# Loading the second block's x behind the first weights, low halves on VectorE, and new transfer durations in a planned decoder layer

## Chip, cores and metric

The kernel runs on one core of a Trainium2 chip. The metric is the device time of one execution in microseconds (us).

## What is computed

One decoder layer on x (2048 x 1024, float32), cut to what matters here:

```python
a = rmsnorm(h, attn_norm)                          # d_model 1024
proj = einsum('bsd,de->bse', a, w_in)              # dq, dk, dv, sq, sk, sv: 512 columns each
diff_o = diff_attn(...)                            # 4 heads, softmax(q1 k1) - lam * softmax(q2 k2)
sb_o = stick_breaking(...)                         # 8 heads, products of (1 - beta) along the keys
h = h + concat(norm(diff_o), norm(sb_o)) @ w_out
m = rmsnorm(h, mlp_norm)
h = h + square(relu(m @ w_up)) @ w_down            # d_ff 4096
out = rmsnorm(h, final_norm)
```

Each float32 operand of a dense product is split into a high and a low half (both float32r), and a product is the three matmuls high x high, high x low, low x high. So every weight tile and every x tile is first split: ScalarE (ACT) copies the rounded high half, another engine subtracts it from the raw tile and leaves the low half.

## The kernel before

The sequence is cut into four blocks of 512 columns, taken in the order 3, 2, 1, 0. `emit_qkv((3, 2), ...)` (lines 641 to 654) makes the projections of blocks 3 and 2, weight by weight: `ORDER` lists 16 tiles of w_qk and 4 steps of w_v, and for the first three tiles (`lag` 3) all of block 3 comes ahead of all of block 2. Attention on these blocks follows, mixed with the projections of blocks 1 and 0, then the output product and the MLP of each block.

- `split_w` (537 to 555) loads a raw weight tile of 128 x 1024 (`x` in the profile), makes its two split tiles (`w`: 512 columns of high halves, 512 of low ones) and stores both in DRAM (`d_w_qk`, `d_w_v`, ...), from where later blocks load them ready. The low half is made by POOL in pieces of 256 columns (line 552).
- `load_x` (577 to 582) loads a block's x as four tiles of 128 x 1024 (`b<-x_T`). `norm_x` (591 to 600) splits each half of such a tile: ACT makes the high half, DVE the low one (`b<-b,g_attn`). `rms` and `rms_row` (609 to 632) square the tiles, add them up, reduce them on PE (`r`) and make the row of reciprocal norms.
- `halves` (565 to 570) gives the tiles of an x block's halves, two views of 512 columns in each tile; `space` (584 to 587) adds half a tile for the block's row.
- `emit_qk` (662 to 679): `product` (24 matmuls of 128x512, `d<-b,w`), then DVE scales the result by the row (`y<-d,b`), ACT makes the high half, DVE the low one (`y<-y`), and two transfers store them.

No instruction is issued where the code calls it. The calls are recorded as units with their dependences, and `Plan.order` (201 to 417) lays them out with a list scheduler in a model of the five engines, with durations from `Plan.duration` (160 to 198). A transfer holds SP for the returned 0.42, moves `u.bytes` at a rate by its row length after the transfers ahead of it, and lands 2.2 after its begin plus that move (lines 365 to 369; all in us). Which spot of SBUF a tile takes, and when, follows from `homes`, `MOST` and `LEAST` (421 to 424, 463 to 465). Dense units may run at most `AHEAD` = 100 ahead of the oldest open one. The order is then issued engine by engine; on the chip each engine and the SP queue take their instructions strictly in that order. All calls go through line 447, so the profile gives them that line and they are told apart by tiles.

At the start the recorded order is: gains, the first weight tile, x of block 3, the other two first weights, constants (with `lqk`, the four lambda vectors), and x of block 2 inside `emit_qkv` at step 1 (`load_to(2)`, line 1079), split at step 2 (`norm_to`).

Two lines that the text speaks of:

```python
for i in range(0, BW, HW):                                                   # 551, in split_w
    pool.tensor_tensor(out=lo[:, i:i + HW], in0=r[:, i:i + HW], ...)          # 552
finish = begin + 2.2 + u.moves                                               # 369, in Plan.order
```

Of the kernel before, what the change touches and what calls it, by code (L numbers as in the profile page):

```python
# [28 lines left out]
P = 128  # L29
# [77 lines left out]
class Plan:  # L107
# [52 lines left out]
    def duration(self, eng, method, kw, out, ins, u):  # L160
# [35 lines left out]
        u.bytes = math.prod(out.shape) * 4  # L196
        u.moves = u.bytes / {P: 265e3, HW: 300e3, BW: 335e3, D: 360e3}.get(row, 200e3)
        return 0.42


    def order(self, slots, phase_of, caps, log=None):
# [101 lines left out]
        while done < len(units):  # L303
# [14 lines left out]
            while progress:  # L318
                progress = False
                for e in avail:  # L320
# [3 lines left out]
                    for u in waiting[e]:  # L324
                        if u.ready > now + 1e-9:
                            continue
                        k = self.key(u, now)
                        if best is not None and k >= best[0]:
                            continue
                        if u.stream == "dense" and u.i > dense[at_dense].i + self.AHEAD:  # L330
                            continue
                        spots, ok = [], True
                        for t in u.allocs:
                            if queue[u.stream, self.line(t)][-1] is not t:
                                ok = False
                                break
                            s = place(t, now)
                            if s is None:
                                ok = False
                                break  # L340
                            spots.append((t, s))
                            if len(u.allocs) > 1:
                                free[s[0]].remove(s[1])
                        if len(u.allocs) > 1:
                            for t, s in spots:
                                free[s[0]].append(s[1])
                        if ok:
                            best = k, u, spots
# [16 lines left out]
                    if e == "SP":  # L365
                        avail[e] = now + u.dur
                        begin = max(now + 0.1, dma_free)
                        dma_free = begin + u.moves
                        finish = begin + 2.2 + u.moves
                    else:  # L370
                        finish = start + u.dur
                        avail[e] = finish
                        if e == "PE":
                            if now > self.pe_end + 0.05:
                                gaps.append((now - self.pe_end, now, u))
                            self.pe_end = finish
# [13 lines left out]
                    for s in u.succ:  # L390
                        s.ndeps -= 1
                        s.ready = max(s.ready, finish if s.eng == e else res + (0.04 if s.eng == "POOL" else 0.0))
                        if not s.ndeps:
                            waiting[s.eng].append(s)
                            heapq.heappush(events, s.ready)
                            if s.eng == "PE":
                                heapq.heappush(events, s.ready + self.MARGIN)
                    for t in users.get(id(u), ()):
                        t.left -= 1
# [18 lines left out]

    MARGIN, AHEAD, pe_end = 0.4, 100, 0.0

# [11 lines left out]
    def key(self, u, now):  # L432
# [3 lines left out]
        if u.eng == "SP":  # L436
            return (u.stream == "dense", u.frac if u.stream != "dense" else u.n)

# [13 lines left out]
def layer_kernel(ctx: ExitStack, tc: tile.TileContext, a: dict, out: bass.AP):  # L452
# [9 lines left out]
    TINY = dict(rvx=2, rrx=2, rx=4, rvh=2, rrh=2, negm=2, l=2, gam=2, rl=2, mm=2, left=8)  # L462
    homes = {"be": ["early", "xp"], "we": ["early"], "ye": ["early"], "xe": ["early"], "e": ["e", "e2"], "bx": ["xp"], "b": ["late", "xp"], "w": ["late", "xp"], "y": ["late", "xp"],
             "x": ["late", "xp"], "wm": ["xp"], "ym": ["m", "xp"], "xm": ["xp"], "yq": ["m", "xp"], "wq": ["xp"]}
# [72 lines left out]
    def split_w(name, *at):  # L537
# [9 lines left out]
        for j, t in enumerate(tiles):  # L547
            r, hi, lo = raw[:, j * BW:(j + 1) * BW], t[:, 0:BW], t[:, BW:D]
            act.activation(out=hi, in_=r, func=ACTF.Copy)

            for i in range(0, BW, HW):
                pool.tensor_tensor(out=lo[:, i:i + HW], in0=r[:, i:i + HW], in1=hi[:, i:i + HW].bitcast(F32), op=ALU.subtract)
            kept[name, at].append(dt(f"d_{name}_{'_'.join(map(str, at))}_{j}", [P, D]))
# [11 lines left out]
    def halves(last=False):  # L565
# [3 lines left out]
        h = h[0::2], h[1::2]  # L569
        return h, ([h[0][k // 2][:, k % 2] for k in range(KD)], [h[1][k // 2][:, k % 2] for k in range(KD)], b_)  # L570

# [12 lines left out]
    def space(last=False):  # L584
        n = len(rows) % 2
        rows.append(rows[-1] if n else buf(last=last))
        return halves(last) + (rows[-1][:, n * BW:(n + 1) * BW],)
# [3 lines left out]
    def norm_x(xs, where):  # L591

        tiles, views, row = where
        for kp, x in enumerate(xs):
            for k in range(2):
                g = g_attn[:, 2 * kp + k:2 * kp + k + 1]
                x_, hi, lo = x[:, k * BW:(k + 1) * BW], tiles[0][kp][:, k], tiles[1][kp][:, k]
                act.activation(out=hi, in_=x_, func=ACTF.Copy, scale=g)
# [431 lines left out]

    nxt = {}

# [26 lines left out]
    for i, n in enumerate(("lambda_q1", "lambda_k1", "lambda_q2", "lambda_k2")):  # L1059
# [18 lines left out]

    emit_qkv((3, 2), xs, 3, {1: load_to(2), 2: norm_to(2, False), 12: load_to(1), 13: norm_to(1, True),
                             16: load_to(0), 18: norm_to(0, True)}, ws)  # L1080
# [25 lines left out]
    slots.update(m=["m0", "m1"], e2=[f"f{i}" for i in range(4)])  # L1106
    phases = {k: ["be", "we", "ye", "xe"] for k in [*ATT, "m"]}
    phases.update(e2=["yq", "ym"], late=list(ATT))
# [80 lines left out]
```

## Time and profile before

| | |
|---|---|
| median of 3 runs | 2978.68 us (2973.56 to 2979.01) |
| the profiled execution | 2972.79 us, of which 2971.0 us is the span from first to last instruction |
| PE matmul busy | 2892.6 us, 97% of the span |
| DVE / ACT / POOL busy | 1767.4 (59%) / 1146.2 (39%) / 1099.7 us (37%) |
| DMA | 667.80 MB over one hardware queue, 67.5% of 16 engines' span |
| granted TensorE clock | 0.991 on average |

PE is TensorE, DVE is VectorE, POOL is GpSimd, SP issues all transfers. A row of the timeline gives start, length, engine, instruction, count, and in brackets how long the engine had been idle and what released it. A busy PE is modelled from pipelined matmuls.

### The profile page before, as it was taken

How to read it: one execution, taken by the hardware profiler on the slowest of the kernel's cores; microseconds unless marked ns; L12 is line 12 of the kernel's file. 1: busy time of each engine (PE TensorE's matmuls, PEld its weight loads, DVE VectorE, ACT ScalarE, POOL GpSimd, SP SyncE). 2: the span in 40 equal slices, each digit the busy share in tenths (PEclk: the TensorE clock that was granted, in tenths of full speed). 3: DMA queues.
4: the chain of work that ended last, by engine and by line, in shares of the span. 5: the costliest groups of instructions: out<-in, count | busy, mean ns of one | idle time of the engine just before them, and what ended most of it. 6: DMA issues, size and time to landing. Idle time of an engine off the chain costs nothing.

```text
span 2971.0 us, 42391 instructions
## 1 busy us (share of the span) xinstructions
PE 2892.6 (97%) x14928; PEld 2439.6 (82%) x14928; DVE 1767.4 (59%) x3193; ACT 1146.2 (39%) x2390; POOL 1099.7 (37%) x1589
## 2 busy tenths in 40 slices
PE   8999999999999999999999999999999999999997
PEld 6889789888887888788788888888888888888886
DVE  5243477777777888884588888887443333421112
ACT  4232255555655555663355555553120100211101
POOL 3221266554677787775344444543000000000000
PEclk9999999999999999999999999999999999999998
DMA  8776897777887877678866665654865556645551
GB/s 268 246 245 202 259 270 233 218 218 230 264 269 244 262 255 254 238 250 288 308 216 204 198 189 192 215 186 169 325 244 200 183 184 241 255 143 205 205 185 71
DMA packets 304164, 670.51 MB, mean 226 GB/s; under 512 B 26960, under 2 KB 121424, under 8 KB 303952
## 3 DMA queue, kind: packets, MB, share of 16 engines
q1 hardware_dynamic: 303952, 667.80, 67.5%
q8 instruction: 119, 1.95, 0.3%
q14 instruction: 93, 0.76, 0.1%
HBM read 491.53 MB, written 176.16 MB: 225 GB/s over the span
## 4 chain that ended last, share of the span: by engine, by line
PE 88%; DMA 6%; DVE 2%; POOL 1%; issue 1%; ACT 1%; SPq 1%; POOLq 0%; DVEq 0%; ACTq 0%
PE d L447 43%; PE dn L447 23%; PE s L447 8%; PE pt L447 6%; PE os L447 4%; PE od L447 3%; DMA v<-d_dv 2%; DMA sq<-d_sq 1%; DMA b<-x_T 1%; SPq L447 1%; DMA qa<-d_dq 1%; DVE b L447 1%; PE r L447 0%; POOL set L447 0%; POOL w L447 0%
## 5 line engine op out<-in xcount | busy, mean ns | idle before, releaser
L447 PE MATMUL d<-b,w 128*128 128x512 f32 x5376 | 1300.9, 395 | 14.1 <-ACT b L447 11.7
L447 PEld LDWEIGHTS d<-b,w 128*128 128x128 f32 x5376 | 1005.3, 189 | 233.1 <-ACT b L447 12.3
L447 PE MATMUL dn<-y,w 128*128 128x512 f32 x3072 | 742.3, 394 | 1.5 <-DVE y L447 1.4
L447 PEld LDWEIGHTS dn<-y,w 128*128 128x128 f32 x3072 | 572.9, 188 | 129.1 <-DVE y L447 1.7
L447 DVE TENSOR_TENSOR b<-b,dn 128x512 f32<-128x512 f32 x416 | 284.8, 685 | 294.9 <-PE dn L447 289.7
L447 POOL TENSOR_TENSOR w<-x,w 128x256 fp32r<-128x256 f32 x384 | 321.8, 860 | 254.5 <-ACT w L447 190.0
L447 POOL TENSOR_TENSOR set<-ser 128x512 f32<-128x512 f32 (+2 forms) x320 | 308.4, 965 | 153.3 <-DVE ser L447 139.7
L447 POOL TENSOR_TENSOR rrx<-rvx,mhalf 128x4 f32<-128x4 f32 x12 | 13.0, 1085 | 880.6 <-DVE rvx L447 880.6
L447 ACT ACTIVATE d<-d 128x512 f32<-128x512 f32 x128 | 74.9, 585 | 596.2 <-DVE d L447 595.8
L447 DVE SCALAR_TENSOR_TENSOR d<-d,b 128x512 f32<-128x512 f32 x128 | 89.3, 698 | 345.8 <-PE d L447 338.2
L447 DVE TENSOR_TENSOR_SCAN ser<-set,left 128x512 f32<-128x512 f32 x192 | 271.8, 1419 | 4.1 <-POOL set L447 3.0
L447 ACT ACTIVATE e<-e,negm 128x512 f32<-128x512 f32 (+3 forms) x320 | 210.5, 658 | 144.3 <-DVE negm L447 134.2
L447 ACT ACTIVATE hb<-pt 128x512 fp32r<-128x512 f32 (+1 forms) x320 | 163.7, 533 | 228.4 <-PE pt L447 135.9
L447 DVE TENSOR_TENSOR hb<-pt,hb 128x512 fp32r<-128x512 f32 (+1 forms) x320 | 186.6, 603 | 54.1 <-ACT hb L447 49.7
L447 DVE CUSTOM_DVE_ANT_0 e<-s,bias 128x512 f32<-128x512 f32 (+3 forms) x320 | 191.4, 598 | 39.4 <-PE s L447 38.9
L447 POOL TENSOR_SCALAR set<-set 128x512 f32<-128x512 f32 (+1 forms) x160 | 120.5, 754 | 240.6 <-ACT set L447 240.2
L447 ACT ACTIVATE set<-s 128x512 f32<-128x512 f32 (+1 forms) x320 | 165.5, 535 | 106.4 <-PE s L447 87.7
L447 PE MATMUL d<-w,b 128*128 128x256 f32 x1536 | 200.9, 285 | 3.3 <-DVE y L447 1.7
L447 PEld LDWEIGHTS d<-w,b 128*128 128x128 f32 x1536 | 190.5, 190 | 8.8 <-DVE y L447 5.1
L447 PE MATMUL s<-ka,qa 128*128 128x512 f32 (+3 forms) x640 | 178.5, 377 | 17.3 <-issue 8.2
L447 PE MATMUL os<-hb,sv 128*128 128x512 f32 (+3 forms) x640 | 186.3, 373 | 5.0 <-DVE hb L447 3.9
L447 PE MATMUL s<-ska,sq 128*128 128x512 f32 (+3 forms) x640 | 181.6, 379 | 7.6 <-DMA sq<-d_sq 3.8
(91 smaller groups left out, 3037.5 us busy)
## 6 DMA issues: line engine op xcount, KB each, us to landing
w<-d_w_up SPq DMA_DIRECT2D x192, 512.0 KB, 5.5
w<-d_w_down SPq DMA_DIRECT2D x192, 512.0 KB, 5.0
ka<-d_dk SPq DMA_DIRECT2D x80, 512.0 KB, 5.4
v<-d_dv SPq DMA_DIRECT2D x144, 256.0 KB, 4.3
d_w_up<-w SPq DMA_DIRECT2D x64, 512.0 KB, 5.4
d_w_down<-w SPq DMA_DIRECT2D x64, 512.0 KB, 6.2
w<-d_w_out SPq DMA_DIRECT2D x48, 512.0 KB, 6.9
ska<-d_sk SPq DMA_DIRECT2D x80, 256.0 KB, 4.1
```

The costliest lines, as they stand in the source:

```text
L447: fn(*[v.ap() if isinstance(v, View) else v for v in args], **{k: v.ap() if isinstance(v, View) else v for k, v in kw.items()})
```

## The change

- `load_x(2)` is recorded right behind the splits of the first three weights, instead of at step 1 of `emit_qkv`; `norm_to(2)` stays at step 2.
- While the weights' home is still the early one (all of `emit_qkv((3, 2), ...)`), their low halves are made by DVE, in one piece of 512 columns, instead of by POOL in two of 256. Later weights stay with POOL.
- The tile with the rows of blocks 3 and 2 gets a line of its own, `re`, in the early part of SBUF.
- `halves` cuts its views as plain column slices, whose columns the planner sees, where it did not through the rearranged views; `norm_x` uses these views.
- The planner's durations of a transfer: SP is held 0.48 instead of 0.42, the rates are some 6 to 11% lower, the landing is 2.6 instead of 2.2 behind.
- Three new numbers, `STORE`, `LOAD` and `EARLY`, enter the rules with values (0.0, 0.0, and 100 like `AHEAD`) that leave them as they were.

```diff
@@ -194,8 +194,8 @@
             return 0.19 + n * 0.00085
         row = min([out.shape[-1]] + [v.shape[-1] for v in ins])
         u.bytes = math.prod(out.shape) * 4
-        u.moves = u.bytes / {P: 265e3, HW: 300e3, BW: 335e3, D: 360e3}.get(row, 200e3)
-        return 0.42
+        u.moves = u.bytes / {P: 250e3, HW: 270e3, BW: 300e3, D: 320e3}.get(row, 200e3)
+        return 0.48
 
 
     def order(self, slots, phase_of, caps, log=None):
@@ -324,10 +324,12 @@
                     for u in waiting[e]:
                         if u.ready > now + 1e-9:
                             continue
+                        if e == "SP" and u.out.home is None and now < u.ready + self.STORE:
+                            continue
                         k = self.key(u, now)
                         if best is not None and k >= best[0]:
                             continue
-                        if u.stream == "dense" and u.i > dense[at_dense].i + self.AHEAD:
+                        if u.stream == "dense" and u.i > dense[at_dense].i + (self.AHEAD if len(self.seen) > 1 else self.EARLY):
                             continue
                         spots, ok = [], True
                         for t in u.allocs:
@@ -366,7 +368,7 @@
                         avail[e] = now + u.dur
                         begin = max(now + 0.1, dma_free)
                         dma_free = begin + u.moves
-                        finish = begin + 2.2 + u.moves
+                        finish = begin + 2.6 + u.moves
                     else:
                         finish = start + u.dur
                         avail[e] = finish
@@ -395,6 +397,9 @@
                             heapq.heappush(events, s.ready)
                             if s.eng == "PE":
                                 heapq.heappush(events, s.ready + self.MARGIN)
+                            if s.eng == "SP":
+                                heapq.heappush(events, s.ready + self.STORE)
+                                heapq.heappush(events, s.ready + self.LOAD)
                     for t in users.get(id(u), ()):
                         t.left -= 1
                         for kind in gate.get(t.home, ()):
@@ -416,7 +421,7 @@
         self.report = dict(end=max(u.finish for u in units), busy=busy, gaps=gaps)
         return out
 
-    MARGIN, AHEAD, pe_end = 0.4, 100, 0.0
+    MARGIN, AHEAD, pe_end, STORE, LOAD, EARLY = 0.4, 100, 0.0, 0.0, 0.0, 100
 
     MOST = {("be", "xp"): 7, ("we", "early"): 8, ("xe", "early"): 4, ("w", "xp"): 6, ("x", "xp"): 2, ("y", "xp"): 6,
             ("wm", "xp"): 4, ("wq", "xp"): 5, ("xm", "xp"): 2, ("ym", "xp"): 6, ("x", "late"): 4, ("w", "late"): 12}
@@ -434,7 +439,7 @@
             late = u.ready + self.MARGIN > now
             return (late, u.stream == "dense", u.frac if u.stream != "dense" else u.n)
         if u.eng == "SP":
-            return (u.stream == "dense", u.frac if u.stream != "dense" else u.n)
+            return (u.ready + self.LOAD > now, u.stream == "dense", u.frac if u.stream != "dense" else u.n)
 
         return u.ready - (10.0 if u.psum else 0.0)
 
@@ -460,7 +465,7 @@
 
     ATT = dict(qa=1, ka=2, e=12, v=2, ha0=2, ha1=2, fa=3, sq=1, ska=1, sv=1, set=8, ser=2, hb0=2, hb1=2, fb=2, osb=1)
     TINY = dict(rvx=2, rrx=2, rx=4, rvh=2, rrh=2, negm=2, l=2, gam=2, rl=2, mm=2, left=8)
-    homes = {"be": ["early", "xp"], "we": ["early"], "ye": ["early"], "xe": ["early"], "e": ["e", "e2"], "bx": ["xp"], "b": ["late", "xp"], "w": ["late", "xp"], "y": ["late", "xp"],
+    homes = {"re": ["early"], "be": ["early", "xp"], "we": ["early"], "ye": ["early"], "xe": ["early"], "e": ["e", "e2"], "bx": ["xp"], "b": ["late", "xp"], "w": ["late", "xp"], "y": ["late", "xp"],
              "x": ["late", "xp"], "wm": ["xp"], "ym": ["m", "xp"], "xm": ["xp"], "yq": ["m", "xp"], "wq": ["xp"]}
     homes.update({k: [k] for k in [*ATT, *TINY] if k not in homes})
     plan = Plan(homes)
@@ -548,8 +553,10 @@
             r, hi, lo = raw[:, j * BW:(j + 1) * BW], t[:, 0:BW], t[:, BW:D]
             act.activation(out=hi, in_=r, func=ACTF.Copy)
 
-            for i in range(0, BW, HW):
-                pool.tensor_tensor(out=lo[:, i:i + HW], in0=r[:, i:i + HW], in1=hi[:, i:i + HW].bitcast(F32), op=ALU.subtract)
+            for i in range(0, BW, BW if home[0] == "be" else HW):
+                c = slice(i, i + (BW if home[0] == "be" else HW))
+                (vec if home[0] == "be" else pool).tensor_tensor(out=lo[:, c], in0=r[:, c], in1=hi[:, c].bitcast(F32),
+                                                                 op=ALU.subtract)
             kept[name, at].append(dt(f"d_{name}_{'_'.join(map(str, at))}_{j}", [P, D]))
             dma(kept[name, at][j], t)
         return Weights(tiles)
@@ -567,7 +574,7 @@
         b_ = [buf(F32R, last) for _ in range(KD)]
         h = [t.rearrange("p (k s) -> p k s", k=2) for t in b_]
         h = h[0::2], h[1::2]
-        return h, ([h[0][k // 2][:, k % 2] for k in range(KD)], [h[1][k // 2][:, k % 2] for k in range(KD)], b_)
+        return h, tuple([b_[2 * (k // 2) + j][:, k % 2 * BW:(k % 2 + 1) * BW] for k in range(KD)] for j in range(2)) + (b_,)
 
     def x_pair():
         t = buf(F32R, kind=2)
@@ -583,7 +590,7 @@
 
     def space(last=False):
         n = len(rows) % 2
-        rows.append(rows[-1] if n else buf(last=last))
+        rows.append(rows[-1] if n else buf(last=last) if last else tile_view("re", [P, D], F32, "b"))
         return halves(last) + (rows[-1][:, n * BW:(n + 1) * BW],)
 
     rows = []
@@ -594,7 +601,7 @@
         for kp, x in enumerate(xs):
             for k in range(2):
                 g = g_attn[:, 2 * kp + k:2 * kp + k + 1]
-                x_, hi, lo = x[:, k * BW:(k + 1) * BW], tiles[0][kp][:, k], tiles[1][kp][:, k]
+                x_, hi, lo = x[:, k * BW:(k + 1) * BW], views[0][2 * kp + k], views[1][2 * kp + k]
                 act.activation(out=hi, in_=x_, func=ACTF.Copy, scale=g)
                 vec.scalar_tensor_tensor(out=lo, in0=x_, scalar=g, in1=hi.bitcast(F32), op0=ALU.mult, op1=ALU.subtract)
         return views + ([], lambda: rms(xs, row))
@@ -1028,7 +1035,7 @@
     for e in starts[1:]:
         ws[e] = [split_w("w_qk", e)]
 
-    nxt = {}
+    nxt = {2: load_x(2)}
 
     def load_to(b):
         def f():
@@ -1076,7 +1083,7 @@
     vec.tensor_scalar(out=neglam, in0=neglam, scalar1=-LAM_INIT, scalar2=None, op0=ALU.add)
 
 
-    emit_qkv((3, 2), xs, 3, {1: load_to(2), 2: norm_to(2, False), 12: load_to(1), 13: norm_to(1, True),
+    emit_qkv((3, 2), xs, 3, {2: norm_to(2, False), 12: load_to(1), 13: norm_to(1, True),
                              16: load_to(0), 18: norm_to(0, True)}, ws)
     home[:] = ["b", "wq", "yq", "xm"]
     emit_attention(3)
@@ -1104,7 +1111,7 @@
                  psum=[f"p{i}" for i in range(8)])
     slots.update({k: [f"{k}{i}" for i in range(n)] for k, n in [*ATT.items(), *TINY.items()]})
     slots.update(m=["m0", "m1"], e2=[f"f{i}" for i in range(4)])
-    phases = {k: ["be", "we", "ye", "xe"] for k in [*ATT, "m"]}
+    phases = {k: ["be", "we", "ye", "xe", "re"] for k in [*ATT, "m"]}
     phases.update(e2=["yq", "ym"], late=list(ATT))
 
     def caps(kind, plan):
```

The planner's order moves all along the program. Three places of it follow. First SP's queue at the start. `x<-w_qk` is a raw weight tile, `b<-x_T` is x (the first four tiles are block 3's, the second four block 2's), `d_w_qk...<-w` stores a split weight. Before, from the second store on:

```order
L447 DMA d_w_qk_1_179<-w 128x1024
L447 DMA b<-lambda_q 128x64
L447 DMA g_sb<-sb_subln 64x1
L447 DMA d_w_qk_0_181<-w 128x1024
L447 DMA b<-lambda_k 128x64
L447 DMA d_w_qk_1_182<-w 128x1024
L447 DMA b<-lambda_q 128x64
L447 DMA d_w_qk_0_183<-w 128x1024
L447 DMA b<-lambda_k 128x64
L447 DMA d_w_qk_1_184<-w 128x1024
L447 DMA x<-w_qk 128x1024
L447 DMA b<-x_T 128x1024 x4
```

and in the change:

```order
L452 DMA g_diff_187<-diff_subln 128x1
L452 DMA d_w_qk_0_178<-w 128x1024
L452 DMA d_w_qk_1_179<-w 128x1024
L452 DMA g_sb<-sb_subln 64x1
L452 DMA b<-x_T 128x1024 x4
L452 DMA b<-lambda_q 128x64
L452 DMA d_w_qk_0_181<-w 128x1024
L452 DMA d_w_qk_1_182<-w 128x1024
L452 DMA d_w_qk_0_183<-w 128x1024
L452 DMA d_w_qk_1_184<-w 128x1024
```

The x of block 2 stood behind all six stores of the first split weights and the lambda vectors; now only the first weight's two stores stand ahead of it, and the other four stores and the lambda vectors behind it.

Second, DVE's first rows in the change (`w<-x,w` are the weights' low halves, `b<-b,g_attn` x's low halves, `b<-b` sums of squares):

```order
L452 TENSOR_TENSOR w<-x,w 128x512 x2
L452 SCALAR_TENSOR_TENSOR b<-b,g_attn 128x512 x7
L452 TENSOR_TENSOR b<-b 128x1024
L452 SCALAR_TENSOR_TENSOR b<-b,g_attn 128x512
L452 TENSOR_TENSOR b<-b 128x1024
L452 TENSOR_TENSOR w<-x,w 128x512 x2
L452 TENSOR_SCALAR g_diff<-g_diff_187 128x1
L452 TENSOR_TENSOR w<-x,w 128x512 x2
L452 TENSOR_TENSOR b<-b 128x1024
L452 TENSOR_TENSOR b<-b 128x512
L452 SCALAR_TENSOR_TENSOR b<-b,g_attn 128x512 x3
L452 TENSOR_SCALAR rvx<-r 128x4
```

Before, DVE had none of the `w<-x,w` rows (they were 128x256 rows of POOL) and began with the seven `b<-b,g_attn`; block 2's came behind the three `y<-d,b` of block 3.

Third, PE at a place of the attention, ahead of a diff head's first scores (`s<-ka,qa`; `s<-ska,sq` are the other kind's scores, `d<-b,w` a dense product). Before:

```order
L447 MATMUL s<-ska,sq 128x512 x6
L447 MATMUL d<-b,w 128x512 x8
L447 MATMUL r<-ident,b 128x128 x4
L447 MATMUL d<-b,w 128x512 x8
L447 MATMUL s<-ka,qa 128x512 x4
```

and the end of the same piece for the same head in the change, where the six `s<-ska,sq`, four `r`, 16 `d` and 16 transposes `pt` stand ahead of it:

```order
L452 MATMUL os<-hb_10437,sv 128x512
L452 MATMUL os<-hb_10458,sv 128x512
L452 MATMUL s<-ska,sq 128x512 x2
L452 MATMUL os<-hb_10445,sv 128x512
L452 MATMUL os<-hb_10460,sv 128x512
L452 MATMUL s<-ska,sq 128x384 x2
L452 MATMUL s<-ska,sq 128x256 x2
L452 MATMUL d<-b,w 128x512 x8
L452 MATMUL os<-hb_10478,sv 128x512
L452 MATMUL os<-hb_10501,sv 128x512
L452 MATMUL s<-ska,sq 128x128 x2
L452 MATMUL s<-ka,qa 128x512 x2
```

The transfers of that head's `qa` stand, in both, behind those of `sq`, which wait for the six `s<-ska,sq`; between these and the first use of `qa` lay 20 matmuls, and now 58.

## Rows read from the trace of the kernel before

**Rows 1.** The page: the span, and the first row of part 1.

```profile
span 2971.0 us, 42391 instructions
...
PE 2892.6 (97%) x14928; PEld 2439.6 (82%) x14928; DVE 1767.4 (59%) x3193; ACT 1146.2 (39%) x2390; POOL 1099.7 (37%) x1589
```

**Rows 2.** Busy time by stretch: length, engines' busy us (instructions), PE clock, DMA, GB/s.

```profile
7.17:29.65 22.48, 21.26 (x84) 16.02 (x84) 13.98 (x19) 10.84 (x17) 11.72 (x11) 1.00 0.77 284
29.65:57.67 28.02, 22.32 (x85) 17.25 (x85) 16.82 (x22) 14.62 (x23) 11.13 (x13) 0.82 0.86 280
...
300.00:1800.00 1500.00, 1454.01 (x8022) 1244.40 (x8021) 1137.87 (x2179) 790.79 (x1748) 882.93 (x1292) 0.99 0.76 243
...
2952.00:2971.00 19.00, 3.94 (x17) 2.93 (x15) 8.66 (x14) 1.65 (x2) 1.01 (x1) 0.59 0.29 110
```

**Rows 3.** Timeline of PE at the start: start, length, instruction, count, idle before.

```profile
7.17 0.79 PE L447 MATMUL d<-b,w 128*128 128x512 f32 x1 [7.17 <-ACT b L447]
...
27.56 2.09 PE L447 MATMUL d<-b,w 128*128 128x512 f32 x8
34.20 0.80 PE L447 MATMUL d<-b,w 128*128 128x512 f32 x1 [4.55 <-ACT b L447]
...
57.67 53.75 PE L447 MATMUL d<-b,w 128*128 128x512 f32 x232
```

**Rows 4.** Timeline of SP's queue at the start.

```profile
10.57 0.57 SPq L447 DMA_DIRECT2D g_sb<-sb_subln  x1
11.75 1.59 SPq L447 DMA_DIRECT2D d_w_qk<-w  x2
14.37 0.33 SPq L447 DMA_DIRECT2D b<-lambda_q  x1
...
24.54 3.02 SPq L447 DMA_DIRECT2D b<-x_T  x4
```

**Rows 5.** Timeline of DVE and POOL at the start.

```profile
5.65 3.23 POOL L447 TENSOR_TENSOR w<-x,w 128x256 fp32r<-128x256 f32 x4 [4.49 <-ACT w L447]
...
7.16 4.92 DVE L447 SCALAR_TENSOR_TENSOR b<-b,g_attn 128x512 fp32r<-128x512 f32 x6 [7.16 <-ACT b L447]
...
12.52 0.75 DVE L447 SCALAR_TENSOR_TENSOR b<-b,g_attn 128x512 fp32r<-128x512 f32 x1 [0.45 <-ACT b L447]
13.47 1.23 DVE L447 TENSOR_TENSOR b<-b 128x1024 f32<-128x1024 f32 x1 [0.20 <-ACT b L447]
14.04 8.99 POOL L447 TENSOR_TENSOR w<-x,w 128x256 fp32r<-128x256 f32 x8 [5.16 <-ACT w L447]
```

**Rows 6.** Groups of instructions by form, 0 to 300 us: count, busy us, mean ns.

```profile
L447 POOL TENSOR_TENSOR w<-x,w 128x256 fp32r<-128x256 f32 x96 | 80.2, 868 | 171.7 <-ACT w L447 123.3 <-DVE y L447 29.1 <-DMA d_dq<-y 10.7
...
L447 DVE TENSOR_TENSOR y<-y 128x512 fp32r<-128x512 f32 x32 | 23.9, 756 | 18.5 <-ACT y L447 18.4
```

**Rows 7.** Two stretches at a lower granted clock, columns as in rows 2.

```profile
900.70:907.40 6.70, 3.28 (x8) 2.63 (x9) 3.64 (x6) 0.92 (x3) 2.76 (x3) 0.50 1.06 316
33.70:43.90 10.20, 8.55 (x18) 5.90 (x19) 7.64 (x9) 7.69 (x11) 3.49 (x4) 0.50 0.95 281
```

**Rows 8.** Waits of PE, 300 to 1850 us: total us, times, longest.

```profile
PE s L447 <- issue: 8.2, 3, 5.5
PE s L447 <- DMA qa<-d_dq: 7.2, 4, 3.9
PE od L447 <- DMA v<-d_dv: 6.1, 8, 1.7
...
PE s L447 <- DMA sq<-d_sq: 3.8, 4, 1.6
```

**Rows 9.** Transfers by name: count, size, median us from issue to landing.

```profile
v<-d_dv SPq DMA_DIRECT2D x144, 256.0 KB, 4.3
...
qa<-d_dq SPq DMA_DIRECT2D x64, 256.0 KB, 5.8
```

**Rows 10.** Timeline of SP's queue at the place in the attention.

```profile
890.38 0.58 SPq L447 DMA_DIRECT2D qa<-d_dq  x1
...
896.49 0.58 SPq L447 DMA_DIRECT2D qa<-d_dq  x1
```

**Rows 11.** Timeline of PE there.

```profile
904.12 2.04 PE L447 MATMUL s<-ka,qa 128*128 128x512 f32 x4 [5.47 <-issue]
```

## The prediction

> **What bounds the kernel now.** I read the page first: PE is busy 2892.6 of 2971.0 us [rows 1], every other engine 59% or less. So the time is PE's work plus the 78.4 us in which PE stands idle, plus what a lower clock adds; another engine matters only where PE waits for it. Next, the table by stretch [rows 2] shows where the idle time lies. Length minus PE busy gives 1.2 us from 7.17 to 29.65, 5.70 us from 29.65 to 57.67, 46.0 us in the attention from 300 to 1800 and 15.1 us in the last 19 us; 7.17 us pass before the first matmul [rows 3], and some 3 us are scattered. Then the timelines of PE and SP at the start say why the second stretch is bad, and the list of PE's waits says what the 46 us consist of. The profiled execution took 2972.79 us, 5.9 less than the median of the runs shown (2978.68); I make the sum against the first and add 5.9 at the end. A measurement of this kernel can tell some 0.2%, 6 us, from no change.
>
> **Part 1: block 2's x loaded earlier.** PE ends block 3's three products at 27.56 + 2.09 = 29.65 and starts block 2's at 34.20, after 4.55 us idle [rows 3]. It waits for ACT's first high half of block 2, and that for the load: the four `b<-x_T` are issued from 24.54 on [rows 4], behind six stores that wait for POOL's low halves, whose last eight pieces run from 14.04 to 23.03 [rows 5]. From that issue to the first matmul it is 34.20 - 24.54 = 9.7 us. In the changed order the four loads stand right behind two stores and `g_sb`. The entry at that place is now issued at 14.37 [rows 4]; I take this as the new issue, since those two stores wait for low halves that DVE has by about 7.2 (below). 14.4 + 9.7 = 24.1 us, 5.5 us ahead of 29.65, so the load is off the path even if it is some us late. What the stretch gains:
>
> - Its idle time, 28.02 - 22.32 = 5.70 us [rows 2].
> - The clock. Right after the idle time the granted clock is 0.50, that is 1.2 GHz in place of 2.4, from 33.7 to 43.9 [rows 7]. The 18 matmuls there took 8.55 busy us. At the full-clock rate of 53.75 / 232 = 0.232 us [rows 3] they take 4.2, so 4.4 us go, if PE comes to block 2 without a pause.
>
> Together 10.1 us. Bounds: 0, if the load or its splitting is still late; 11, if block 3's 1.2 us go too.
>
> What moves behind the loads is the lambda vectors and four stores. DVE waits for the former at its lambda product, which now stands behind block 3's three y; nobody on PE's path needs the product before the attention. The stores free split tiles later, but the weights behind them are consumed only after the first 144 dense matmuls, at about 46 us. I cost both at nothing; the cover is those 144 matmuls, and if it failed, the wait would be for the fourth weight.
>
> **Part 2: low halves on DVE.** POOL loses 96 pieces of 868 ns, 80.2 us up to 300 us; DVE gains 48 of 128x512. The trace has no such instruction of DVE on a weight; the nearest row is the same subtraction with the same tile shape, `y<-y`, 756 ns [rows 6]. I take 0.756, so 48 x 0.756 = 36.3 us of DVE. From above it is bounded by 1.23 us, the 128x1024 sum [rows 5], from below by nothing known short of half of that, 0.6. Is it on the path? The first two halves can start where POOL's did, at 5.65, and end at 5.65 + 1.51 = 7.16, just when x's first low half starts now [rows 5]: cost 0. Then DVE has eight x halves of 0.75 and two or three sums of 1.23 [rows 5] before the second and third weight: 7.16 + 6.0 + 2.5 = 15.6, low halves at 16.4 and 17.1, then 18.7 for the third weight. PE needs the second weight's when block 3's first product ends, about 17 now. From 7.16 on, DVE's list up to the last low half of block 2 is 16 x 0.75 + 4 x 0.756 + 5 x 1.23 = 21.2 us, plus about 1 for the norm: it ends near 30, where PE begins to need the eight halves one by one, every 3 x 0.232 = 0.7 us. That is cover, but thin: I take +1.5 us as the price, between 0 and 4. After the start the steady stretch needs per weight 48 matmuls, 11.1 us of PE, against two low halves and at most four y instructions of DVE, 6 x 0.756 = 4.5 us: covered.
>
> Own place for the rows, and views by plain slices: no work is added. The slices let ACT make a tile's second high half without waiting for the first low one; that lies inside block 3's 1.2 us. Cost 0.
>
> **Part 3: the planner's transfer durations.** No instruction gets longer; the order changes, so that more work stands between a transfer's release and its use. What it can give back is PE's waiting for transfers in the attention. The list has 7.2 us for `qa`, 6.1 for `v`, 3.8 for `sq`, and 8.2 for "issue", of which one wait is 5.5 [rows 8]. That one ends at 904.12 [rows 11], 7.6 us after the second half of `qa` was issued at 896.49, itself 6.1 us behind the first half [rows 10]; a `qa` load takes 5.8 us by its median [rows 9], so I count it as a transfer. Sum 5.5 + 7.2 + 6.1 + 3.8 = 22.6 us. The old plan lands a `v` load of 262144 bytes in 0.1 + 262144/300000 + 2.2 = 3.2 us, the new one in 3.7; the trace says 4.3 [rows 9]. So the new value is nearer, and still short.
>
> At the place shown from the order, 20 matmuls stood between the release of the transfers ahead of `qa` and its use, and now 58; at the trace's rate the difference is more than the wait. I take that wait as gone, 5.5 us, and with it the low clock behind it: 8 matmuls took 3.28 us busy [rows 7] and need 1.9, so 1.4 more. Of the other 17.1 us I take half, 8.5, because the plan moved from 1.1 short of the trace to 0.6 short. That is 15.4 us; bounds 0 and 24.0.
>
> A remade order also moves the waits that are not for transfers, 46.0 - 22.6 = 23.4 us. The model for those engines is unchanged, so I take no net change, with half of it, 12 us, on either side at the extremes.
>
> The Trainium skill prices a transfer (DMA: Bandwidth & Descriptors, section "Anatomy of one DMA — SWDGE (gpsimd) path") as a fixed cost of about 2.0 us plus the bytes over 436 GB/s, a fit for another issuing path. By it a `v` load would land in 2.6 us, an estimate, the old plan would already be too long, and the sum would be without part 3 (the second rival). The trace's 4.3 us speaks against it.
>
> The end, 15.1 us idle [rows 2], is the last norm behind the last product; its rows keep their order. Nothing.
>
> **Sum.** -10.1 + 1.5 - 15.4 = -24.0. 2972.8 - 24.0 = 2948.8 in a profile like the one shown; plus 5.9 it is 2954.7, and I say 2954.
>
> **Rivals.**
> 1. Only the start gains: -10.1 + 1.5 = -8.6, 2970 on the median's scale. The longer plan only spaces out its loads, and the waits return under other names. For it: many loads have a single buffer and follow the use of the one before. Against it: the place shown. Chance 0.16, most of it still faster.
> 2. The remade order pays it back: the 23.4 us of other waits grow by 12, and of part 3 only the one place stays: -8.6 - 6.9 + 12 = -3.5, 2975. Chance 0.09, no change.
> 3. Slower: DVE's low halves become the path of the projections. DVE takes its list in order; a low half that stands behind a step which waits for PE (the norm's `rvx`, a y) makes PE wait for the weight. If each of the 48 cost its 0.756, it would be +36.3 - 10.1, 2999 in the profile, 3005 on the median's scale. It decides if DVE's work per weight passes the 11.1 us that PE needs; 4.5 speaks against it, and so does DVE's 16.82 busy us in the 28.02 us of the worst stretch [rows 2]. Chance 0.05.
>
> **Numbers.** The forecast has 0.70. Faster by over 0.2%: 0.70 and 0.14 of rival 1, 0.84. Within 0.2%: 0.09 and the 0.02 left of rival 1, 0.11. Slower: 0.05. The range goes from all transfer waits gone and a few us of the others too (-10.1 - 24.0 - 6 = -40, 2938) up to rival 1 and a little past it, 2972; rivals 2 and 3 stay outside.
>
> **What the profile will show.** Right: PE goes from block 3's 72 matmuls into block 2's without a pause at about 29 us at full clock, and is done with both near 47 in place of 57.67; four `b<-x_T` issued near 14 to 17; DVE near full up to 30 us, with `w<-x,w` around 0.7 us each; PE idle from 300 to 1800 near 33 us, less of it for `qa` and `v`. Wrong: idle time of PE before 50 us released by DVE `w` or `b`, or a low clock there (part 1 or 2); attention idle still 46 (rival 1) or more (rival 2); idle time between 57 and 300 us (rival 3).

## The result

The changed kernel takes 2942.1 us (median of 6 runs, 2933.83 to 2944.88) against 2976.12 us before (6 runs in the same comparison, 2969.78 to 2983.14): a ratio of 0.9884, 95% interval 0.9864 to 0.9903, 34 us less. Forecast were 24 us less, 2954 us, in a range of 2938 to 2972. Its profile is of its fastest execution, 2933.83 us, with a span of 2931.9 us; so differences of single profiles below are larger than those of the medians.

The stretches of [rows 2] in the changed kernel (length, then PE, PEld, DVE, ACT, POOL busy, PE clock, DMA share, GB/s; the last stretch is the end):

```profile
7.17:29.65 22.48, 21.36 (x88) 16.63 (x89) 20.36 (x30) 19.04 (x29) 1.02 (x1) 1.00 0.96 356
29.65:57.67 28.02, 28.02 (x130) 23.03 (x129) 17.07 (x32) 10.19 (x18) 1.01 (x1) 1.00 0.83 282
...
300.00:1800.00 1500.00, 1476.06 (x8175) 1262.71 (x8174) 1168.17 (x2237) 806.17 (x1787) 908.40 (x1311) 1.00 0.76 246
...
2913.00:2931.90 18.90, 3.78 (x20) 2.66 (x18) 8.66 (x14) 1.65 (x2) 1.01 (x1) 0.67 0.29 111
```

The idle time between 29.65 and 57.67, 5.70 us before, is 0, at full clock; that of the attention fell from 46.0 to 23.9 us; the end is the same.

The start, PE's timeline (answers to [rows 3]):

```profile
7.24 7.36 PE L452 MATMUL d<-b,w 128*128 128x512 f32 x22 [7.24 <-ACT b L452]
...
16.84 5.30 PE L452 MATMUL d<-b,w 128*128 128x512 f32 x22 [0.55 <-DVE w L452]
...
28.40 0.60 PE L452 MATMUL r<-ident,b 128*128 128x128 f32 x4
28.76 9.49 PE L452 MATMUL d<-b,w 128*128 128x512 f32 x40
...
43.04 57.12 PE L452 MATMUL d<-b,w 128*128 128x512 f32 x248
```

PE goes from block 3 into block 2 at 28.76 without a pause. The first three weights take six products on the two blocks, 144 dense matmuls in all. Before, these were done by 57.67; now 128 are done by 43.04. I therefore compare the start of the 145th, which is 43.04 plus 16 matmuls, 46.8 us: 10.9 us earlier. SP's queue and DVE there (answers to [rows 4] and [rows 5]):

```profile
13.06 0.56 SPq L452 DMA_DIRECT2D g_sb<-sb_subln  x1
14.47 1.77 SPq L452 DMA_DIRECT2D b<-x_T  x4
```

```profile
5.81 1.29 DVE L452 TENSOR_TENSOR w<-x,w 128x512 fp32r<-128x512 f32 x2 [5.81 <-ACT w L452]
7.22 2.08 DVE L452 SCALAR_TENSOR_TENSOR b<-b,g_attn 128x512 fp32r<-128x512 f32 x3
...
28.44 1.23 DVE L452 TENSOR_TENSOR b<-b 128x1024 f32<-128x1024 f32 x1
29.67 1.90 DVE L452 SCALAR_TENSOR_TENSOR y<-d,b 128x512 f32<-128x512 f32 x3
```

The x of block 2 is issued at 14.47, 10 us earlier, and DVE's list of halves and sums ends at 29.67, nearly without a break.

In the attention, the largest waits of PE from 300 to 1850 us and all for transfers (answers to [rows 8]):

```profile
PE pt L452 <- POOL set L452: 4.7, 4, 2.5
PE os L452 <- DVE hb L452: 4.4, 3, 3.1
PE s L452 <- DMA qa<-d_dq: 2.9, 4, 1.4
...
PE os L452 <- DMA sv<-d_sv: 0.8, 2, 0.6
PE s L452 <- DMA ska<-d_sk: 0.8, 2, 0.5
...
PE s L452 <- issue: 0.4, 1, 0.4
...
PE od L452 <- DMA v<-d_dv: 0.2, 1, 0.2
```

For transfers (with "issue") it is 5.1 us, where the four rows shown of before alone had 25.3 and the whole list 30.8 (31.6 up to 2800 us). "Issue" may be counted so: by the trace each of the three such waits before ends 0.09 us after a `qa` load has landed, the longest at 904.12 after a landing at 904.03. The low clock in the middle of the program falls from 27.3 us in five pieces to 13.7 in three.

### The profile page after: what moved, and what is told of

Its sections match the earlier page's. It is cut to its first block, busy times and chain, and to the rows that moved or that the text cites. A ratio compares the mean times of both kernels' runs of the same rounds, so it can differ in the third digit from the quotient of the medians.

```text
span 2931.9 us, 42252 instructions
## 1 busy us (share of the span) xinstructions
PE 2881.6 (98%) x14928; PEld 2433.0 (83%) x14928; DVE 1788.4 (61%) x3241; ACT 1143.9 (39%) x2390; POOL 1028.9 (35%) x1493
## 4 chain that ended last, share of the span: by engine, by line
PE 92%; DMA 3%; DVE 2%; ACT 1%; issue 1%; SPq 0%; POOL 0%; POOLq 0%; DVEq 0%; ACTq 0%
PE d L452 46%; PE dn L452 24%; PE s L452 8%; PE pt L452 7%; PE os L452 4%; PE od L452 3%; DMA qa<-d_dq 1%; DVE b L452 1%; PE r L452 0%; DMA sv<-d_sv 0%; DMA b<-x_T 0%; SPq L452 0%; DVE ser L452 0%; DMA x<-w_down 0%; ACT b L452 0%
## 5 line engine op out<-in xcount | busy, mean ns | idle before, releaser
L452 POOL TENSOR_TENSOR set<-ser 128x512 f32<-128x512 f32 (+2 forms) x320 | 317.5, 994 | 129.3 <-DVE ser L452 121.9
L452 POOL TENSOR_TENSOR w<-x,w 128x256 fp32r<-128x256 f32 x288 | 241.8, 858 | 83.9 <-ACT w L452 75.6
L452 PE MATMUL s<-ska,sq 128*128 128x512 f32 (+3 forms) x640 | 175.7, 375 | 1.3 <-DMA ska<-d_sk 0.8
```

Of the source, the lines that this page charges most:

```text
L452: fn(*[v.ap() if isinstance(v, View) else v for v in args], **{k: v.ap() if isinstance(v, View) else v for k, v in kw.items()})
```

## Experiments

Four measures stand for each run: the median and its ratio to the kernel before in the same comparison, the start of the 145th dense matmul, and PE's idle time past 300 us without the end, split into waits for transfers (with "issue") and for other engines (sums of the lists of waits, which leave out the shortest ones: 46.6 of 47.5 us before). The last three are from one profiled execution each, and single executions of one kernel lie up to 18 us apart, so only large steps in them count. The kernel before was run anew with each four; its medians there are 2976.35 to 2978.0 us, and the ratio is to these. The plain slices of `halves` have no run of their own; e1 and e5 show the two gains without them.

| run | median us | ratio (95%) | 145th at us | idle past 300: transfers + others |
|---|---|---|---|---|
| before | 2976.12 | 1 | 57.7 | 31.6 + 15.0 |
| changed | 2942.10 | 0.9884 (0.9864 to 0.9903) | 46.8 | 5.1 + 18.2 |
| e1_durations_only | 2945.23 | 0.9886 (0.9870 to 0.9902) | 53.7 | 5.9 + 18.9 |
| e2_all_but_durations | 2974.45 | 0.9975 (0.9962 to 0.9989) | 46.5 | 26.9 + 25.5 |
| e3_early_load_only | 2982.36 | 1.0018 (1.0006 to 1.0030) | 53.3 | 28.4 + 25.1 |
| e5_own_row_only | 2967.95 | 0.9968 (0.9956 to 0.9980) | 47.5 | 31.8 + 18.0 |
| e6_changed_late_x | 2942.23 | 0.9878 (0.9861 to 0.9894) | 47.0 | 8.6 + 19.8 |
| e7_changed_pool_low | 2935.78 | 0.9850 (0.9829 to 0.9872) | 46.7 | 2.6 + 22.1 |
| e8_longer_landing (3.0) | 2931.43 | 0.9844 (0.9827 to 0.9861) | 46.6 | 10.5 + 14.1 |
| e9_longest_landing (3.4) | 2925.61 | 0.9826 (0.9808 to 0.9843) | 47.0 | 4.0 + 17.4 |
| e10_rates_and_hold_only | 2938.06 | 0.9872 (0.9856 to 0.9888) | 46.7 | 19.1 + 12.0 |
| e11_landing_only | 2956.80 | 0.9938 (0.9921 to 0.9956) | 46.2 | 24.1 + 16.7 |
| e12_landing_4_2 | 2917.12 | 0.9801 (0.9786 to 0.9816) | 46.7 | 0.4 + 14.3 |
| e13_pool_low_landing_3_4 | 2959.53 | 0.9941 (0.9926 to 0.9956) | 47.1 | 6.6 + 31.8 |

### The durations alone, and all but them

```diff
-        u.moves = u.bytes / {P: 265e3, HW: 300e3, BW: 335e3, D: 360e3}.get(row, 200e3)
-        return 0.42
+        u.moves = u.bytes / {P: 250e3, HW: 270e3, BW: 300e3, D: 320e3}.get(row, 200e3)
+        return 0.48
...
-                        finish = begin + 2.2 + u.moves
+                        finish = begin + 2.6 + u.moves
```

> The kernel before with the new transfer durations alone (0.48, lower rates, 2.6). In its order the x of block 2 still stands behind all the stores of the first weights. Theory (the start's gain comes from the early x, the attention's from the durations): the 145th dense matmul starts near 57 us as before (changed kernel 46.8), the idle time of PE past 300 us falls from 47.5 us to about 25 (changed kernel 24.3), with less low clock; 20 to 27 us faster. Rival (any remade order would have done it, or the durations need the other parts): idle past 300 us between 35 and 60, within 8 us of before.

The second run is the changed kernel with these lines turned back:

> The changed kernel with the planner's old transfer durations (0.42, old rates, 2.2). Theory: the start keeps its gain (145th dense matmul at 46 to 48 us), idle time of PE past 300 us goes back to about 47 us with some 20 us or more of it for transfers; 8 to 14 us faster than before. Rival (any remade order gives it): idle past 300 us near 25 as in the changed kernel, 30 us faster or more.

The durations alone bring 2945.23 us, 33 us less; all the rest without them 2974.45, by the ratio 7 us less. The first is beyond its expected gain (20 to 27), helped by a start that its remade order also makes 4 us earlier; the second keeps the start's 11 us and falls just short of its 8 to 14. The largest waits of PE from 300 to 1850 us in the run without the new durations, and below them the largest and those for `sv` and `v` in the run with the durations alone:

```profile
PE s L452 <- issue: 6.7, 3, 4.4
PE pt L452 <- DVE e L452: 4.8, 5, 2.9
PE s L452 <- DMA sq<-d_sq: 4.6, 5, 1.7
PE os L452 <- DMA sv<-d_sv: 4.3, 3, 2.0
```

```profile
PE r L447 <- DVE b L447: 4.3, 3, 2.5
...
PE os L447 <- DMA sv<-d_sv: 1.8, 1, 1.8
...
PE od L447 <- DMA v<-d_dv: 1.2, 2, 0.9
```

In the first list the names differ from [rows 8], and the sum for transfers stays near that of before (26.9 against 31.6). "Any remade order would do it" falls: four different orders with the old durations have 26.9 to 31.8 us of transfer waits, four with the new ones 2.6 to 8.6.

### Early load alone, own row alone, and the changed kernel with a late recording

```diff
-    nxt = {}
+    nxt = {2: load_x(2)}
...
-    emit_qkv((3, 2), xs, 3, {1: load_to(2), 2: norm_to(2, False), 12: load_to(1), 13: norm_to(1, True),
+    emit_qkv((3, 2), xs, 3, {2: norm_to(2, False), 12: load_to(1), 13: norm_to(1, True),
```

> The kernel before with the x of block 2 recorded early, and nothing else; low halves stay with POOL. Theory (the start's gain is the early x): no pause of 4.5 us between the blocks and no low clock there, 145th dense matmul at 47 to 50 us; 7 to 11 us faster from the start, with the attention's idle time near 47 and whatever the remade order adds or takes there. Rival (without DVE's low halves the weights of POOL hold the start back): 145th dense matmul past 53 us.

```diff
-        rows.append(rows[-1] if n else buf(last=last))
+        rows.append(rows[-1] if n else buf(last=last) if last else tile_view("re", [P, D], F32, "b"))
```

(with `re` added to the homes and to the tiles that the attention's part of SBUF waits for)

> The kernel before with the own place for the row tile alone; x of block 2 is recorded where it was, the low halves stay with POOL, the durations are the old ones. Theory (the x was held back in the planner by the row's tile, which stands ahead of it in the same line of tiles and is only taken at the norm): the x moves up in SP's queue as it does with the early recording, and the 145th dense matmul starts at 47 to 50 us. Rival (the place of the row is worth nothing, as the prediction had it): 57 us as before.

The third is the changed kernel with the first diff above turned back:

> The changed kernel with the x of block 2 recorded where it was before (step 1 of the projections); own row, DVE's low halves and new durations stay. Theory (own row alone frees the x, the early recording is a second way to the same): x still issued by about 15 to 18 us, 145th dense matmul at 46 to 49 us, within 5 us of the changed kernel. Rival (the recording's place is what counts): x behind the stores, 145th past 52 us, 5 us or more slower than the changed kernel.

The early recording alone is no gain: 2982.36 us, the 145th matmul at 53.3. That meets the number of its rival (past 53), but not the rival's reason: the own row alone reaches 47.5 with all low halves on POOL. The x is issued at 15.07, but SP, DVE and PE show why that does not help (the three timelines of this run):

```profile
15.07 1.92 SPq L447 DMA_DIRECT2D b<-x_T  x4
```

```profile
28.57 1.91 DVE L447 SCALAR_TENSOR_TENSOR y<-d,b 128x512 f32<-128x512 f32 x3 [3.08 <-ACT b L447]
30.39 0.74 DVE L447 SCALAR_TENSOR_TENSOR b<-b,g_attn 128x512 fp32r<-128x512 f32 x1
```

```profile
31.19 0.73 PE L447 MATMUL d<-b,w 128*128 128x512 f32 x2 [1.22 <-DVE b L447]
...
34.53 10.09 PE L447 MATMUL d<-b,w 128*128 128x512 f32 x36 [1.70 <-DVE b L447]
```

With x long there, DVE still makes block 2's first low half only behind block 3's y, after 3.08 us of waiting for the row. The own row alone brings the 145th matmul to 47.5 us and 2967.95 us, with x recorded where it was and all low halves on POOL. Its timelines of SP, DVE and PE:

```profile
14.78 2.81 SPq L447 DMA_DIRECT2D b<-x_T  x4
```

```profile
29.65 0.75 DVE L447 SCALAR_TENSOR_TENSOR b<-b,g_attn 128x512 fp32r<-128x512 f32 x1
...
32.79 1.88 DVE L447 SCALAR_TENSOR_TENSOR y<-d,b 128x512 f32<-128x512 f32 x3
```

```profile
43.68 20.71 PE L447 MATMUL d<-b,w 128*128 128x512 f32 x89
```

The x is issued as early as with the early recording, and now DVE has the last low half of block 2 before block 3's y. And with the own row, the recording's place is worth nothing: 2942.23 us and 47.0.

So it was the row. The code says how: tiles of one home are handed out in the order in which the recorded program first uses them. The row of block 3 is first used in its first `emit_qk`, recorded ahead of `load_to(2)` and `norm_to(2)`, but can be written only when the norm is through PE. As long as the row was a `be` tile, block 2's x (before) or its halves (early load alone) stood behind it in that line.

### Low halves back on POOL

```diff
-            for i in range(0, BW, BW if home[0] == "be" else HW):
-                c = slice(i, i + (BW if home[0] == "be" else HW))
-                (vec if home[0] == "be" else pool).tensor_tensor(out=lo[:, c], in0=r[:, c], in1=hi[:, c].bitcast(F32),
-                                                                 op=ALU.subtract)
+            for i in range(0, BW, HW):
+                pool.tensor_tensor(out=lo[:, i:i + HW], in0=r[:, i:i + HW], in1=hi[:, i:i + HW].bitcast(F32), op=ALU.subtract)
```

> The changed kernel with all low halves back on POOL. The run with the early load alone lost 6 us of its start to waits for DVE and ACT while POOL worked beside. Theory (DVE's low halves are worth some us at the start only, since POOL's pieces come later and slow DVE beside them): 145th dense matmul at 48 to 53 us in place of 46.8, the attention as in the changed kernel (idle past 300 us 20 to 30), 2 to 7 us slower than the changed kernel. Rival (worth nothing or a cost): 145th at 47 us or before.

Missed: 2935.78 us, no slower than the changed kernel (the intervals meet), the 145th matmul at 46.7. The rival holds: moving the low halves to DVE is worth nothing here. With the landing at 3.4 as well (in the changed kernel's line `finish = begin + 2.6 + u.moves`), to see whether the two gains add up:

> The changed kernel with POOL's low halves and the landing at 3.4, each of which alone was faster than the changed kernel (6 and 16 us). Theory (POOL's halves cost nothing once x is early and leave DVE free): start as with either (145th dense matmul near 47 us), 2922 to 2930 us. Rival (POOL's 6 us were the remade order's): 2930 us or more, or start past 49 us.

It is 2959.53 us. The start is as good, but PE's waits past 300 us have other heads:

```profile
PE pt L452 <- DVE e L452: 9.6, 6, 4.4
PE os L452 <- DVE hb L452: 4.3, 7, 1.0
PE pt L452 <- DVE hb L452: 4.2, 1, 4.2
```

31.8 us of waits that are not for transfers, where all other runs have 12.0 to 25.5. That is what a remade order can take, the mechanism of the second rival. With orders this far apart, the 6 us by which POOL's low halves alone were faster can't be put down to the halves. Nor is a longer landing a gain in every order: with the low halves on POOL, 2.6 gave 2935.78 and 3.4 gives 2959.53, 24 us more.

Of the 31.8 us, the two longest waits, 4.2 and 4.4, stand behind one DVE instruction each. For the first, DVE, POOL and PE show:

```profile
1046.91 4.24 DVE L452 SCALAR_TENSOR_TENSOR e<-e,gam 128x256 f32<-128x256 f32 x1
...
1047.42 3.44 POOL L452 TENSOR_TENSOR w<-x,w 128x256 fp32r<-128x256 f32 x5
...
1051.81 0.73 PE L452 MATMUL pt<-ident,set 128*128 128x128 f32 x4 [4.23 <-DVE hb L452]
```

The median `e<-e,gam` of this run takes 0.75 us. Here one takes 4.24 and, before 1114.27, another 5.35, each while POOL goes from one instruction to the next without a break, and each ends within 0.6 us of the end of POOL's row. The longest wait of the run with POOL's low halves alone (4.1 us, at 881.6) stands behind a third such case, of 4.40 us. The `w<-x,w` pieces here are of later weights, which POOL splits in every version. That POOL held DVE is read from these three cases; no run tests it. The rest of the 31.8 us is open.

### More, and parts, of the durations

```diff
-                        finish = begin + 2.6 + u.moves
+                        finish = begin + 3.0 + u.moves
```

and the same with 3.4 and 4.2; then with 2.2, so that only rates and SP's 0.48 are new; and the 2.6 with the old rates and 0.42.

> The changed kernel with the planner's landing 3.0 in place of 2.6. In the changed kernel's trace PE still waits some 5 us for transfers past 300 us. Theory (the gain grows with the planned landing until the loads are covered, then stops): idle past 300 us 18 to 25, 0 to 5 us faster than the changed kernel. Rival (planned too long, loads and their buffers hold the attention back): idle above 30, slower.

> The changed kernel with the landing at 3.4. Theory: transfers' waits near nothing, other waits near 18, within 5 us of the changed kernel. Rival (planned too long): idle above 30 us and slower by 5 us or more.

> The changed kernel with the landing at 4.2. At 3.0 and 3.4 it was still 10 and 16 us faster than the changed kernel. Theory (covered by now; what is left is waits for other engines): idle past 300 us 18 to 25, within 5 us of the run at 3.4. Rival (now planned too long: single buffers hold the attention back, or the start's loads are put off): slower than at 3.4 by more than 5 us.

> The changed kernel with the landing back at 2.2; the lower rates and the 0.48 of SP stay. With all three old, idle time past 300 us was 53.2 us (24.3 in the changed kernel). Theory (the landing is the larger part for loads of 256 KB: 0.4 us against 0.1 for the rate): idle 38 to 50, 10 to 25 us slower than the changed kernel. Rival (SP's hold and the rates do it): idle 20 to 30, within 6 us of the changed kernel.

> The changed kernel with the old rates and the old 0.42 of SP, and the new landing of 2.6. Theory (landing): idle past 300 us 25 to 35, 0 to 10 us slower than the changed kernel. Rival (SP's hold and the rates): idle 45 or more, 20 us slower.

With the landing at 3.0, 3.4 and 4.2 the medians are 2931.43, 2925.61 and 2917.12 us: the gain goes on past what was expected, and with DVE's low halves "planned too long" does not show. By the formula of the prediction a `v` load is then planned at 4.1, 4.5 and 5.3 us, where the trace of before has 4.3. That fewer waits for transfers are what each step gained is shown only in part: at 3.0 the profile has 10.5 us of them, more than the changed kernel's 5.1. At 4.2 the list of waits from 300 to 1850 us has hardly a transfer; its first rows:

```profile
PE pt L452 <- DVE fb L452: 2.1, 1, 2.1
PE pt L452 <- DVE e L452: 2.0, 2, 1.3
PE pt L452 <- POOL set L452: 1.9, 2, 1.0
```

This is the best version: 0.9801 of before. Of the parts, the rates and SP's 0.48 alone leave 19.1 us of transfer waits and the landing alone 24.1, against 5.1 with both. In time the first is level with the changed kernel (2938.06), the second 15 us slower. The expectation that the landing is the larger part fell; the level medians do not speak against the 14 us more of transfer waits: the first run's profile is of its slowest execution, 2943.27 us, the changed kernel's of its fastest, 2933.83, and these 9.4 us agree with 14 us more for transfers and 6 us less for others. So the waits of a single profile are uncertain by several us, and 19.1 and 24.1 can't be told apart by them. The medians can: against the run with all three durations old (ratio 0.9975), rates and SP's hold alone bring 31 us, the landing alone 11, all three 27.

## Why the prediction was right, and where it was wrong

**The bound.** Right: PE's work stayed, its idle time and the low clock behind it went. The 39.1 us between the spans, 2971.0 and 2931.9, are 10.9 up to the 145th dense matmul and 28.2 behind it: 23.2 of idle time (47.5 to 24.3) and most of the rest the low clock, 13.6 us less of it at half speed.

**Part 1, the size.** Right within 1 us: 10.1 forecast, 10.9 measured, no pause and no low clock (rows above). The derived issue at 14.4 came at 14.47, the 145th matmul near 47 at 46.8.

**Part 1, the cause.** Wrong. The prediction gave this to the early recording and to stores that DVE's low halves let go sooner, and put the own place of the row at cost 0, with no gain. The runs show the reverse: the own row alone does it (47.5), the recording alone does not (53.3), and taken back it costs nothing (47.0). The stores ahead of x in SP's queue were where the delay showed, not what made it. The size could come right all the same, because it was read from the planner's new order, whichever of the edits had made that order.

**Part 2, the price of DVE's low halves.** Sized at +1.5 us; measured 0 in the start. The nearest row served: 686 ns against the 756 taken. The answer to [rows 6]:

```profile
L452 DVE TENSOR_TENSOR w<-x,w 128x512 fp32r<-128x512 f32 x48 | 31.6, 686 | 13.1 <-ACT w L452 13.0
...
L452 DVE SCALAR_TENSOR_TENSOR b<-b,g_attn 128x512 fp32r<-128x512 f32 x32 | 22.6, 747 | 1.9 <-ACT b L452 1.5
```

DVE ended its list near 30 as worked out. The third rival, slower by these halves, did not come: PE's idle time from 57.67 to 300 us is 2.6 us.

**Part 3, the size.** The mis-sized term. Taken were 15.4 us: one wait whole, half of the other 17.1. Measured are 26 us fewer of transfer waits (31.6 to 5.1), and 23 to 29 fewer in the four orders with the new durations. That is most of why 34 us came where 24 were forecast. Three steps of the term failed. The 22.6 us left out 9.0 us of waits, listed as `d_dk`, `ska` and the small "issue" ones for the most part, which mostly went too; so the waits for other engines were 15.0 and not 23.4. And "half, because the plan moved from 1.1 short of the trace to 0.6 short" looked at one load by itself, for which the rates change 0.1 us; yet rates and SP's hold alone bring 31 us by the medians and the landing alone 11. In the plan a transfer begins only behind the moves of those ahead of it, so lower rates add up along the queue; that this is the reason is not shown. And the place shown went only in part as said. The scores `s<-ka,qa` do follow without idle time, but some 10 us earlier PE now waits for POOL, and dense matmuls run at half clock behind that (answers to [rows 11], and the stretch from 878.30):

```profile
874.06 0.33 PE L452 MATMUL pt<-ident,set 128*128 128x128 f32 x1 [1.03 <-POOL set L452]
876.92 1.20 PE L452 MATMUL pt<-ident,set 128*128 128x128 f32 x9 [2.53 <-POOL set L452]
877.88 3.46 PE L452 MATMUL d<-b,w 128*128 128x512 f32 x8
...
886.09 0.33 PE L452 MATMUL s<-ska,sq 128*128 128x128 f32 x2
886.26 0.68 PE L452 MATMUL s<-ka,qa 128*128 128x512 f32 x2
```

```profile
878.30:881.60 3.30, 3.30 (x11) 2.52 (x10) 3.30 (x7) 0.59 (x2) 3.13 (x3) 0.50 0.82 154
```

So of the 5.5 us of that wait 3.6 are back under another name, and the 1.4 us for the clock with them: the eight matmuls take 3.46 us and need 1.9. This is what the first rival said of the waits; it came true at this one place and not in the sum.

**The Trainium skill's fit** (DMA: Bandwidth & Descriptors, section "Anatomy of one DMA — SWDGE (gpsimd) path"). By it the old plan was long enough and the durations worth nothing, which is the prediction's first rival (it names the second there). The run with the durations alone is 33 us faster than before, and a landing of 4.2 makes the changed kernel 25 us faster again: for these transfers the measurements decide against its 2.6 us.

**Other waits.** Taken as no net change: 15.0 to 18.2 us here. But 12 us either way was not too wide a bound: in e13 they are 31.8, nearly 17 more than before.

## To carry to other kernels

In a kernel whose order is planned, a transfer's planned duration is best set at or above what the trace shows from issue to landing: too short left the bounding engine waiting for its loads, and longer gained at each of the three steps tried with DVE's low halves. It is no rule for every order: with POOL's low halves the one longer landing tried lost 24 us, and most of the idle time that it added was waits for other engines. When a load is issued late, look first for what it stands behind in the planner's lines of tiles, then at the queue: here one half-used row tile held back a whole block. A remade order moves the waits for other engines by 10 us or more, so a version is judged by its medians and by the kind of wait that it is meant to remove.

## What was not expected of the hardware

PE's granted clock fell to half for 3.4 to 6.8 us at waits of quite different lengths, and the shorter wait had the longer low clock. In the changed kernel it is at half for 6.8 us from 1438.0, in a wait of 1.63 us that ends at 1438.36, and for 3.4 us from 823.6, in a wait of 3.14 us that ends at 824.18 (the granted clock is the third number from the end):

```profile
823.60:827.00 3.40, 2.82 (x7) 2.27 (x8) 3.40 (x6) 0.60 (x1) 3.40 (x5) 0.50 0.91 371
1438.00:1444.80 6.80, 6.16 (x18) 4.95 (x19) 5.87 (x10) 4.30 (x9) 5.50 (x7) 0.50 0.48 144
```

DVE's low halves of x took 747 ns each up to 300 us in the changed kernel and 898 before, when POOL's 96 pieces ran beside them; with these pieces back on POOL in the changed kernel they take 910.
